# GpSimd without weight splits and residual additions, residual eviction in two VectorE steps, and a third of one modulation summed later

## The chip, the cores and the metric

The kernel runs on one core of one Trainium2 chip. The metric is the device time of one execution in microseconds (us). The engines are named as in the profile: PE (TensorE), DVE (VectorE), ACT (ScalarE), POOL (GpSimd) and SP (SyncE, whose queue issues nearly all DMAs).

## The reference

Two blocks in float32 for 256 tokens of width 2048. The first is a mixer (forgetting attention beside a gated linear recurrence) and a mixture of 16384 small experts; the second is a state-space layer and a sparse attention layer. Each sublayer ends in a residual with a gate that comes from a condition vector:

```python
mod = silu(c) @ w_ada + b_ada                       # [1, 6*2048]: sh1, sc1, ga1, sh2, sc2, ga2
h = rmsnorm(x, g_mix) * (1 + sc1) + sh1
x = x + ga1 * hybrid_mixer(h)                       # w_in, attention and recurrence, w_out
h = rmsnorm(x, g_ffn) * (1 + sc2) + sh2
x = x + ga2 * peer(h)                               # w_q, top-k, u (2048x16384), v (16384x2048)
x = rmsnorm(x, g_final)
for layer in (0, 1):                                # condition vector c_2
    shift, scale, gate = split(silu(c_2) @ mod_w[layer] + mod_b[layer], 3)
    if layer == 1:                                  # shared keys and values: kv_mod_w, w_kv
        shared = nsa_shared_kv(modulate(rmsnorm(x, kv_norm_g), ...))
    h = modulate(rmsnorm(x, norm_g[layer]), shift, scale)
    x = x + gate * (s5_mixer(h) if layer == 0 else nsa_mixer(h, shared))
return rmsnorm(x, final_norm_g)
```

## The kernel before

Activations lie transposed, 16 tiles of 128 channels by 256 tokens, in `x`. Each normed input is kept as a high part in the rounded matmul type and the rest (`xs`). Every weight is used in the same two parts: `half` loads 128x1024 of it by a DMA (tile `raw`, 4 buffers, 512 KB), ACT casts it to `wh` (L342), and a subtraction makes the rest `wl` (L346); `wh` and `wl` have 3 buffers each. A block of 128 output channels (`lin_b`) takes two halves and 16 pairs of matmuls: `wh` with both parts of the input (L357, 512 columns) and `wl` with the high part (L358, 256 columns). Peer's second product (`v_group`) and two others run the other way round (L928 to L930).

Who makes `wl` is set by a share: of each four halves `pool_share` go to POOL, the others to DVE. The share is MP = 1 for w_q, w_k, w_v, MP2 = 2 for w_lx and w_ly, MP3 = 1 for w_out, QP = 3 for peer_w_q, UP = 2 for the first four groups of peer_u, and 0 from then on. That makes 92 splits on POOL and 904 on DVE. DVE's splits are traced with a priority that brings them forward.

A residual eviction (`ev_res`, 16 for each of w_out, ssm_w_out, nsa_w_o) has three engines in a row: ACT scales the first PSUM half (L422), DVE adds the scaled second half (L423), POOL adds the sum to `x` (L424). Behind it ACT squares `x` (L435) and POOL adds the squares (L439); the last square goes to PE, which sums over channels (L445), DVE makes the reciprocal root (L452, L460 to L465: 12 steps, each waiting for the one before), and then norms the input of the next product (L473 to L479). No matmul of the next product can start before that.

The modulations (`gemv`) run in the background, a step at each weight load as the rate allows: SP loads 128x1024 of the matrix (`graw`, 2 buffers, L299), and either PE multiplies, or, where a pool was given by `use_pool`, DVE accumulates into `gacc` (L310 the first, L312 the other 15 of a block of 1024 columns). After 16 steps PE sums `gacc` over its partitions. `self.bg` holds them in order: ga1, ffn, ga2 (w_ada), m0, mkv, m1. `pace(label, loads)` spreads what is left over so many loads, `hold` stops at a label, `need(label)` runs the rest at once. m1 belongs to the last layer; its blocks 0 to 3 are shift and scale, blocks 4 and 5 the gate of the last residual. m0, mkv and m1 are summed in the v stage, where DVE also makes 16 tables for the state-space layer.

The code is traced in this order, and a scheduler then sets the order on every engine's queue by priority and its own forecast of times; the engines take their queues in that order.

Of the kernel before, what the change touches and what calls it, by code (L numbers as in the profile page):

```python
# [9 lines left out]
F = mybir.dt.float32  # L10
# [4 lines left out]
OP = mybir.AluOpType  # L15
# [19 lines left out]
MP = 1  # L35
MP2 = 2
MP3 = 1
# [13 lines left out]
VP = 0  # L51
GP = 1, 0, 1
AHEAD = 200
QP = 3
QS = 3
UP = 2
# [100 lines left out]
class K:  # L157
    def __init__(self, tc, A, dbg=None):
        self.tc, self.nc, self.A = tc, tc.nc, A
        self.dbg = dbg or {}  # L160
        self.full = True
        self.nw, self.pool_share, self.srate = 0, 0, 1
        self.bg, self.side, self.par, self.loads = [], [], [], []
        self.loaded, self.gate, self.gp, self.hold, self.mid = None, None, None, None, False
        self.rate, self.owed, self.sowed, self.towed, self.slow = 1.5, 0.0, 0.0, 0.0, None
# [169 lines left out]
    def half(self, src, i):  # L335
        nc = self.nc
        s = self.sb.tile([128, 1024], F, name="raw", tag="raw", bufs=4)
        with self.after(self.gate):
            self.loaded = nc.sync.dma_start(s, src[:, 1024 * i:1024 * i + 1024])
        h = self.sb.tile([128, 1024], R, name="wh", tag="wh", bufs=3)  # L340
        l = self.sb.tile([128, 1024], R, name="wl", tag="wl", bufs=3)
        nc.scalar.copy(h, s)  # L342
        self.nw += 1
        on_pool = self.nw % 4 < self.pool_share
        with self.tc.high_priority(offset=AHEAD):
            (nc.gpsimd if on_pool else nc.vector).tensor_sub(l, s, h.bitcast(F))  # L346
        return h, l
# [205 lines left out]
    def _mixer(self, x):  # L553
# [6 lines left out]
        for n, w, nb in (("m0", "mod_w0", 6), ("mkv", "kv_mod_w", 4), ("m1", "mod_w1", 6)):  # L560
            if self.full or n == "m0":
                t = cp.tile([128, 8 * nb], F, name=n)
                setattr(self, n, t)
                i, m = {"m0": (0, "mod_b_2"), "m1": (48, "mod_b_2"), "mkv": (0, "kv_mod_b_2")}[n]
# [69 lines left out]
        self.pool_share = MP2  # L634
# [65 lines left out]
        self.pool_share = MP3  # L700
# [47 lines left out]
    def _peer(self, x):  # L748
# [41 lines left out]
        self.pool_share, self.srate = QP, QS  # L790
# [168 lines left out]
        self.pool_share, self.srate = UP, US  # L959
        aps = {}  # L960
        for gi in range(ahead):
            if gi == ahead - 1:
                self.pool_share, self.srate = 0, VS
                self.drain(self.side)
                self.need("ga2")
                self.rate = 0.5
                self.use_pool(None)
                ctx.__exit__(None, None, None)
                aps[0] = self.xs()
                self.side.append(mix(0, gq[0], aps[0]))  # L970
            gq.append(u_group(gi))
# [30 lines left out]
        self.pool_share = 0  # L1002
# [385 lines left out]
    def _nsa(self, x):  # L1388
# [78 lines left out]
        for t in range(2):  # L1467
# [8 lines left out]
                                fill=NEG, base=-31, channel_multiplier=1)  # L1476
        csb = self.ph.tile([128, 2, 128], F, name="csb")
# [81 lines left out]
        for h in range(16):  # L1559
# [11 lines left out]
            self.par.append(head(h, qz, q, sz))  # L1571
        self.drain(self.par)
# [41 lines left out]
```

## Time and profile before

| | |
|---|---|
| median of 3 runs | 3625.65 us (3624.92 to 3626.92) |
| profiled execution | 3617.7 us, span 3616.0 us |
| busy over the span | PE 91%, DVE 73%, ACT 47%, POOL 29% |
| granted PE clock, mean | 0.961 of full speed |
| HBM | 229 GB/s over the span |

The stages, by the first and last loads of their weights in the profiled execution: w_q to w_v 98 to 276 us, w_lx and w_ly 278 to 429, w_out 430 to 567, peer_w_q 567 to 680, peer_u from 681, peer_v 1089 to 2365, ssm_u and ssm_z 2368 to 2696, ssm_w_glu 2699 to 2789, ssm_w_out 2792 to 2879, w_kvt and w_kvn 2882 to 3043, nsa_q and nsa_z 3051 to 3480, nsa_w_o 3481 to 3580. A share of busy time over the whole span hides that PE is full in some of these stages and DVE in others.

### The profile page before, as it was taken

Reading aid. Unit: us, or ns where it says so; the run is one execution under the profiler, and the core shown is the slowest. Engines: PE = TensorE matmul, PEld = TensorE weight load, DVE = VectorE, ACT = ScalarE, POOL = GpSimd, SP = SyncE. Lnnn points to the kernel's source line nnn. Section 1 sums busy time; section 2 is a strip of 40 time slices with the busy share of each in tenths; the row PEclk is TensorE's granted clock in tenths of the full one; section 3 lists DMA queues with packets and bytes.
Section 4 is the critical chain, followed back from the end, with each engine's and each line's share of the span. In section 5 each row is a group of like instructions: output and inputs, shape, how many; then the busy total and the mean of one; then the engine's idle time right before and its main releaser. Section 6 shows DMA issues by size and latency. Waiting matters only on the chain.

```text
span 3616.0 us, 50453 instructions
## 1 busy us (share of the span) xinstructions
PE 3294.4 (91%) x18446; PEld 2726.2 (75%) x18446; DVE 2652.5 (73%) x4072; ACT 1700.7 (47%) x2789; POOL 1066.7 (29%) x892
## 2 busy tenths in 40 slices
PE   4988778999999999999999989988989989999998
PEld 1676666878777777777777777767878878888886
DVE  4778987997657778887777767779886565666665
ACT  1534544455544444554444433354545544555553
POOL 1123345666522121211211233035452320122223
PEclk7999989999999999999999999989999999999999
DMA  9697676567779888888888878744435556444444
GB/s 398 235 301 252 203 234 228 163 223 262 243 250 314 300 281 291 293 285 279 293 286 278 293 268 269 267 158 139 147 127 186 186 167 198 160 155 149 159 143 144
DMA packets 260409, 832.47 MB, mean 230 GB/s; under 512 B 25792, under 2 KB 66880, under 8 KB 257472
## 3 DMA queue, kind: packets, MB, share of 16 engines
q1 hardware_dynamic: 258096, 829.11, 68.0%
q8 instruction: 145, 2.38, 0.3%
q14 instruction: 104, 0.85, 0.1%
q10 hardware_dynamic: 2064, 0.13, 0.0%
HBM read 797.56 MB, written 31.59 MB: 229 GB/s over the span
## 4 chain that ended last, share of the span: by engine, by line
PE 46%; DVE 14%; DMA 13%; issue 6%; POOL 3%; ACT 1%; SPq 0%; DVEq 0%; POOLq 0%; ACTq 0%
PE p L357 22%; PE p L358 11%; DVE wl L346 5%; DMA graw<-mod_w 5%; DMA graw<-kv_mod_w 3%; PE pm L929 2%; PE pm L928 2%; PE pm L930 2%; DVE gacc L312 2%; DMA s5d<-tb 2%; DMA raw<-peer_u 1%; DVE xs L1286 1%; PE pm L882 1%; ACT wh L342 1%; POOL xs L913 1%
## 5 line engine op out<-in xcount | busy, mean ns | idle before, releaser
L357 PE MATMUL p<-xs,wh 128*128 128x512 f32 x5600 | 2038.6, 406 | 43.5 <-DVE xs L476 19.9
L358 PE MATMUL p<-xs,wl 128*128 128x256 f32 x5600 | 1595.6, 285 | 47.6 <-DVE wl L346 40.4
L342 ACT CAST wh<-raw 128x1024 fp32r<-128x1024 f32 x996 | 1038.4, 1048 | 1124.6 <-PE p L357 408.9
L346 DVE TENSOR_TENSOR wl<-raw,wh 128x1024 fp32r<-128x1024 f32 x904 | 1151.4, 1281 | 511.0 <-ACT wh L342 501.4
L357 PEld LDWEIGHTS p<-xs,wh 128*128 128x128 f32 x5600 | 1069.5, 191 | 321.1 <-issue 39.0
L358 PEld LDWEIGHTS p<-xs,wl 128*128 128x128 f32 x5600 | 1078.4, 193 | 74.5 <-DVE wl L346 58.3
L312 DVE SCALAR_TENSOR_TENSOR gacc<-graw,cact,gacc 128x1024 f32<-128x1024 f32 x315 | 448.8, 1425 | 154.5 <-DMA graw<-mod_w 90.2
L929 PE MATMUL pm<-wl,xs 128*128 128x512 f32 x1024 | 411.7, 402 | 25.3 <-DVE wl L346 24.7
L928 PE MATMUL pm<-wh,xs 128*128 128x512 f32 x1024 | 409.4, 400 | 24.2 <-DVE vacc L937 18.8
L930 PE MATMUL pm<-wh,xs 128*128 128x512 f32 x1024 | 405.8, 396 | 0.0
L346 POOL TENSOR_TENSOR wl<-raw,wh 128x1024 fp32r<-128x1024 f32 x92 | 231.8, 2524 | 305.1 <-ACT wh L342 273.1
L909 POOL TENSOR_TENSOR t<-t,t 128x256 f32<-128x256 f32 x128 | 138.3, 1114 | 589.3 <-DMA t<-wd 589.3
L929 PEld LDWEIGHTS pm<-wl,xs 128*128 128x128 f32 x1024 | 196.2, 192 | 85.1 <-DVE wl L346 45.6
L913 POOL TENSOR_TENSOR xs<-t,xs 128x256 fp32r<-128x256 f32 x128 | 150.6, 1207 | 355.0 <-ACT xs L911 354.9
L928 PEld LDWEIGHTS pm<-wh,xs 128*128 128x128 f32 x1024 | 196.0, 191 | 74.9 <-DVE vacc L937 22.1
L930 PEld LDWEIGHTS pm<-wh,xs 128*128 128x128 f32 x1024 | 196.3, 192 | 39.7
L439 POOL TENSOR_TENSOR ssq<-ssq,s 128x256 f32<-128x256 f32 x96 | 105.4, 1107 | 237.7 <-ACT s L435 235.8
L898 ACT ACTIVATE t<-et 128x256 f32<-128x256 f32 x128 | 53.8, 420 | 209.4 <-DVE et L414 209.2
L413 ACT COPY et<-p 128x256 f32<-128x256 f32 x281 | 102.2, 364 | 31.2 <-PE p L358 31.1
L1528 POOL TENSOR_SCALAR t<-t,st 128x128 f32<-128x128 f32 (+1 forms) x64 | 77.6, 1224 | 128.0 <-DVE st L1526 128.0
L872 DVE TENSOR_SCALAR xs<-iof,eT,eT 128x128 f32<-128x128 f32 x192 | 82.2, 487 | 37.9 <-PE pm L882 37.9
L414 DVE TENSOR_TENSOR et<-p,et 128x256 f32<-128x256 f32 x224 | 93.1, 416 | 10.3 <-ACT et L413 10.3
(392 smaller groups left out, 3126.3 us busy)
## 6 DMA issues: line engine op xcount, KB each, us to landing
raw<-peer_u SPq DMA_DIRECT2D x256, 512.0 KB, 5.3
raw<-peer_v SPq DMA_DIRECT2D x256, 512.0 KB, 5.6
graw<-mod_w SPq DMA_DIRECT2D x192, 512.0 KB, 5.6
graw<-w_ada SPq DMA_DIRECT2D x128, 512.0 KB, 4.8
raw<-nsa_z SPq DMA_DIRECT2D x96, 512.0 KB, 3.7
xs<-w_ada SPq DMA_DIRECT2D x16, 2048.0 KB, 13.1
graw<-kv_mod_w SPq DMA_DIRECT2D x64, 512.0 KB, 5.7
raw<-w_out SPq DMA_DIRECT2D x32, 512.0 KB, 5.1
```

What stands on the lines that cost most here:

```text
L312: nc.vector.scalar_tensor_tensor(acc, raw, ck, acc, op0=OP.mult, op1=OP.add)
L342: nc.scalar.copy(h, s)
L346: (nc.gpsimd if on_pool else nc.vector).tensor_sub(l, s, h.bitcast(F))
L357: self.nc.tensor.matmul(p, h[:, sl], x, start=k == 0, stop=False, skip_group_check=True)
L358: self.nc.tensor.matmul(p[:, 1], l[:, sl], x[:, 0], start=False, stop=k == KD - 1, skip_group_check=True)
L413: nc.scalar.copy(t, p[:, 0])
L439: nc.gpsimd.tensor_add(acc[0], acc[0], sq)
L909: nc.gpsimd.tensor_mul(gc, gc, wv[:, c])
L913: nc.gpsimd.tensor_sub(ap[:, c - 2, 1], gs[:, c - 2], ap[:, c - 2, 0].bitcast(F))
L928: nc.tensor.matmul(pp[t], ah, h[:, sl], start=c == 0, stop=False, skip_group_check=True)
L929: nc.tensor.matmul(pp[t], ah, l[:, sl], start=False, stop=False, skip_group_check=True)
L930: nc.tensor.matmul(pp[t], ap[:, c, 1, 128 * t:128 * t + 128], h[:, sl], start=False, stop=c == 7, skip_group_check=True)
```

## The change

POOL makes no `wl` any more: all 996 splits are on DVE, and the shares are gone. A residual eviction is two DVE steps that each add one scaled PSUM half to `x` in place; ACT and POOL have no part in it. Of m1, blocks 4 and 5 get a label of their own, `gate`; it is held back in the v stage, and given free in the last layer, with a pool for its `gacc` there, over 56 loads.

```diff
-MP = 1
-MP2 = 2
-MP3 = 1
-VP = 0
-QP = 3
-UP = 2
...
         nc.scalar.copy(h, s)
-        self.nw += 1
-        on_pool = self.nw % 4 < self.pool_share
         with self.tc.high_priority(offset=AHEAD):
-            (nc.gpsimd if on_pool else nc.vector).tensor_sub(l, s, h.bitcast(F))
+            nc.vector.tensor_sub(l, s, h.bitcast(F))
         return h, l
...
     def ev_res(self, p, x, gate):
         nc = self.nc
-        t, t2 = self.et(), self.et()
-        nc.scalar.activation(t, p[:, 0], AF.Copy, scale=gate)
-        nc.vector.scalar_tensor_tensor(t2, p[:, 1], gate, t, op0=OP.mult, op1=OP.add)
-        nc.gpsimd.tensor_add(x, x, t2)
+        for i in range(2):
+            nc.vector.scalar_tensor_tensor(x, p[:, i], gate, x, op0=OP.mult, op1=OP.add)
...
-                self.bg.append([n, self.gemv(A[w], range(nb), 1, self.col(m, i, 8 * nb), t), 19 * nb + 1])
+            for e, b in ((n, range(nb)),) if n != "m1" else ((n, range(4)), ("gate", range(4, 6))):
+                self.bg.append([e, self.gemv(A[w], b, 1, self.col(m, i, 8 * nb), t), 19 * len(b) + 1])
...
-        if self.full:
-            self.pace("m1", VR)
-        self.pool_share = VP
+        self.pace("m1", VR)
+        self.hold = "gate"
         for gv in range(16):
...
                                 fill=NEG, base=-31, channel_multiplier=1)
+        self.use_pool(self.ph)
+        self.hold = None
+        self.pace("gate", 56)
         csb = self.ph.tile([128, 2, 128], F, name="csb")
...
             self.par.append(head(h, qz, q, sz))
+        self.need("gate")
         self.drain(self.par)
```

The scheduler decides where these steps come to stand. First DVE, at the end of ssm_w_out and the norm that w_kvt waits for (`p` is the PSUM tile of a block, `m` the gate, `s` and `rstd` the tiles of the reciprocal root). Before:

```order
L346 TENSOR_TENSOR wl<-raw,wh 128x1024 x2
L423 SCALAR_TENSOR_TENSOR et<-p_24970,m_993,et 128x256
L452 TENSOR_SCALAR s_25017<-pm 128x256
L460 TENSOR_SCALAR s_25021<-s_25017 128x256
L461 TENSOR_SCALAR rstd<-s_25021 128x256
L463 TENSOR_TENSOR s_25020<-rstd 128x256
```

And of the change, in the same place (lines are those of the changed kernel, some lower than before: L337 is the split, L413 the eviction, L303 and L305 the steps of the modulation):

```order
L413 SCALAR_TENSOR_TENSOR x<-p_24757,m_993,x 128x256 x2
L337 TENSOR_TENSOR wl<-raw,wh 128x1024
L441 TENSOR_SCALAR s_24801<-pm 128x256
L303 TENSOR_SCALAR gacc<-graw,cact 128x1024
L449 TENSOR_SCALAR s_24805<-s_24801 128x256
L305 SCALAR_TENSOR_TENSOR gacc<-graw,cact,gacc 128x1024
L450 TENSOR_SCALAR rstd<-s_24805 128x256
```

Four steps of the gate's second block (L303 and three L305) now stand among the twelve of the reciprocal root; the other twelve stand later, in the norm's end and among the splits of w_kvt. The gate's first block stands earlier than the last layer at all, among the splits of ssm_w_glu, where the queue of before has no such step. DVE of the change there (L405 is an eviction, L1338 belongs to ssm_z):

```order
L1458 MEMSET cm 128x30
L303 TENSOR_SCALAR gacc<-graw,cact 128x1024
L1338 SCALAR_TENSOR_TENSOR t_20235<-et 128x256
L305 SCALAR_TENSOR_TENSOR gacc<-graw,cact,gacc 128x1024
L337 TENSOR_TENSOR wl<-raw,wh 128x1024
L405 TENSOR_TENSOR et<-p_22935,et 128x256
```

All 32 steps of the gate thus left the v stage, and none of them stands in the attention stage proper: PE's sum of the second block is all that comes there. The third place is POOL between w_out and the scores of peer (L424 the residual, L439 the squares, L784 the candidates of the top-k). Before:

```order
L346 TENSOR_TENSOR wl<-raw,wh 128x1024 x2
L424 TENSOR_TENSOR x<-x,et 128x256
L346 TENSOR_TENSOR wl<-raw,wh 128x1024 x4
L784 TENSOR_TENSOR s_5112<-xs 128x256
L346 TENSOR_TENSOR wl<-raw,wh 128x1024 x2
L784 TENSOR_TENSOR s_5177<-xs 128x256
```

And of the change (L428 the squares, L770 the candidates):

```order
L428 TENSOR_TENSOR ssq<-ssq,s_4690 128x256
L428 TENSOR_TENSOR ssq<-ssq,s_4746 128x256
L770 TENSOR_TENSOR s_5064<-xs 128x256
L770 TENSOR_TENSOR s_5129<-xs 128x256
```

The splits stand on DVE now, eight to each four blocks of peer_w_q.

## Rows read from the trace of the kernel before

**Rows 1.** Stretches, all engines: start:end, length, busy us (instructions), clock, DMA, GB/s.
```profile
98.00:302.00 204.00, 183.31 (x1021) 146.62 (x1020) 152.66 (x239) 92.40 (x160) 35.85 (x17) 0.97 0.84 280
302.00:476.00 174.00, 129.94 (x685) 108.84 (x683) 159.43 (x250) 86.61 (x185) 67.54 (x42) 0.90 0.65 212
476.00:586.00 110.00, 88.84 (x488) 74.73 (x489) 85.26 (x95) 45.62 (x72) 59.69 (x38) 0.92 0.77 260
586.00:847.00 261.00, 244.83 (x1529) 205.15 (x1528) 232.79 (x657) 128.57 (x189) 152.86 (x88) 0.96 0.60 199
...
1089.00:2367.00 1278.00, 1202.94 (x5777) 978.40 (x5776) 983.05 (x1076) 571.34 (x760) 262.80 (x231) 0.98 0.84 284
2699.00:2791.00 92.00, 92.00 (x521) 79.62 (x521) 56.31 (x78) 51.02 (x84) 24.15 (x23) 1.00 0.57 183
...
3051.00:3481.00 430.00, 427.04 (x2409) 363.23 (x2408) 269.51 (x483) 229.47 (x500) 93.25 (x87) 1.00 0.48 156
```

The engines of these rows are PE, PEld (weight loads), DVE, ACT, POOL in this order.

**Rows 2.** Splits (L346) by stretch: length, busy us (count) of DVE, POOL.
```profile
98.00:302.00 204.00, 53.33 (x41) 35.46 (x14) 0.97 0.84 280
302.00:476.00 174.00, 20.77 (x18) 44.42 (x16) 0.90 0.65 212
476.00:586.00 110.00, 30.93 (x21) 19.98 (x8) 0.92 0.77 260
586.00:847.00 261.00, 35.43 (x26) 97.30 (x40) 0.96 0.60 199
```

**Rows 3.** DVE lines, 302 to 476 us: busy us, mean ns | idle before.
```profile
L312 DVE SCALAR_TENSOR_TENSOR gacc<-graw,cact,gacc 128x1024 f32<-128x1024 f32 x32 | 58.4, 1826 | 3.1 <-DMA graw<-w_ada 3.1
...
L650 DVE SCALAR_TENSOR_TENSOR s<-lx,cols,s 128x256 f32<-128x256 f32 x24 | 13.5, 565 | 0.2
...
L508 DVE SCALAR_TENSOR_TENSOR et<-et 128x256 f32<-128x256 f32 x8 | 5.3, 668 | 0.6 <-ACT et L507 0.5
...
L512 DVE SCALAR_TENSOR_TENSOR t<-et,t 128x256 f32<-128x256 f32 x8 | 3.3, 412 | 0.0
```

**Rows 4.** Line L312, 98 to 2367 us: shortest/median/longest ns.
```profile
L312 DVE SCALAR_TENSOR_TENSOR gacc<-graw,cact,gacc x315: 1260/1285/3427, 136.1 to 2326.7; 128x1024 f32<-128x1024 f32 x158
```

**Rows 5.** Line L346 on DVE, 2699 to 2897 us, no POOL splits: ns.
```profile
L346 DVE TENSOR_TENSOR wl<-raw,wh x69: 1214/1226/1647, 2702.5 to 2895.1; 128x1024 fp32r<-128x1024 f32 x69
```

**Rows 6.** Line L346 on POOL, whole span: who waited for it (us, times).
```profile
  PEld p L358: 8.1, 5
```

**Rows 7.** Timeline of POOL and of DVE at 430 us: start, length.
```profile
430.59 2.43 POOL L346 TENSOR_TENSOR wl<-raw,wh 128x1024 fp32r<-128x1024 f32 x1 [4.79 <-ACT wh L342]
...
430.68 3.43 DVE L312 SCALAR_TENSOR_TENSOR gacc<-graw,cact,gacc 128x1024 f32<-128x1024 f32 x1
```

**Rows 8.** Groups of the v stage, 1089 to 2367 us: busy, mean | idle before.
```profile
L929 PE MATMUL pm<-wl,xs 128*128 128x512 f32 x1002 | 403.1, 402 | 25.3 <-DVE wl L346 24.7
...
L358 PE MATMUL p<-xs,wl 128*128 128x256 f32 x1304 | 370.9, 284 | 25.5 <-DVE wl L346 25.0
...
L312 DVE SCALAR_TENSOR_TENSOR gacc<-graw,cact,gacc 128x1024 f32<-128x1024 f32 x220 | 295.5, 1343 | 129.5 <-DMA graw<-mod_w 88.0 <-DMA graw<-kv_mod_w 40.2
```

**Rows 9.** Timeline, end of w_out: start, length.
```profile
578.84 4.66 POOL L346 TENSOR_TENSOR wl<-raw,wh 128x1024 fp32r<-128x1024 f32 x2 [0.20 <-ACT wh L342]
...
586.27 1.06 PE L445 MATMUL pm<-s,ones 128*128 128x256 f32 x2
```

**Rows 10.** Timeline, end of ssm_w_out: start, length.
```profile
2896.95 0.70 PE L445 MATMUL pm<-ssq,ones 128*128 128x256 f32 x2
...
2899.04 0.48 DVE L423 SCALAR_TENSOR_TENSOR et<-p,m,et 128x256 f32<-128x256 f32 x1
...
2901.56 0.42 DVE L452 TENSOR_SCALAR s<-pm 128x256 f32<-128x256 f32 x1 [2.04 <-PE pm L445]
```

**Rows 11.** Timeline of DVE, a modulation step inside a reciprocal root.
```profile
478.98 1.28 DVE L312 SCALAR_TENSOR_TENSOR gacc<-graw,cact,gacc 128x1024 f32<-128x1024 f32 x1
480.18 0.42 DVE L463 TENSOR_TENSOR s<-rstd 128x256 f32<-128x256 f32 x1
```

More of the change, by code (lines that the diff above doesn't have):

```diff
@@ L160, in __init__ @@
         self.dbg = dbg or {}
-        self.full = True
-        self.nw, self.pool_share, self.srate = 0, 0, 1
+        self.srate = 1
         self.bg, self.side, self.par, self.loads = [], [], [], []
@@ L560, in _mixer @@
         for n, w, nb in (("m0", "mod_w0", 6), ("mkv", "kv_mod_w", 4), ("m1", "mod_w1", 6)):
[L561 to L564, printed above, removed]
-                self.bg.append([n, self.gemv(A[w], range(nb), 1, self.col(m, i, 8 * nb), t), 19 * nb + 1])
+            t = cp.tile([128, 8 * nb], F, name=n)
+            setattr(self, n, t)
+            i, m = {"m0": (0, "mod_b_2"), "m1": (48, "mod_b_2"), "mkv": (0, "kv_mod_b_2")}[n]
+            for e, b in ((n, range(nb)),) if n != "m1" else ((n, range(4)), ("gate", range(4, 6))):
+                self.bg.append([e, self.gemv(A[w], b, 1, self.col(m, i, 8 * nb), t), 19 * len(b) + 1])
         self.rate, self.hold = R1, "ga2"
-        self.pool_share = MP
         qk = self.xs(F)
@@ L633, in _mixer @@
         self.rate, self.srate = R2, S2
-        self.pool_share = MP2
         lam = self.ph.tile([128, 8], F, name="lam", tag="lam", bufs=1)
@@ L699, in _mixer @@
         self.pace("ffn", 14)
-        self.pool_share = MP3
         for n, p in enumerate(self.lin_bs(A["w_out"], ms, NO)):
@@ L788, in choose @@
                     yield True
-        self.pool_share, self.srate = QP, QS
+        self.srate = QS
         ps = self.lin_bs(A["peer_w_q"], hs)
@@ L958, in _peer @@
         self.side.append(rt)
-        self.pool_share, self.srate = UP, US
+        self.srate = US
         aps = {}
@@ L962, in _peer @@
             if gi == ahead - 1:
-                self.pool_share, self.srate = 0, VS
+                self.srate = VS
                 self.drain(self.side)
@@ L1001, in _peer @@
         self.use_pool(None)
-        self.pool_share = 0
         ctx.__exit__(None, None, None)
```

## The prediction

> **What bounds the kernel now.** I read the stretches of all engines first, since the page's shares (PE 91%, DVE 73%) mix stages with different limits. In [rows 1] PE is busy 244.8 of 261 us in peer_w_q with the top-k, 1202.9 of 1278 in the v stage, all 92 in ssm_w_glu and 427 of 430 in the attention stage: there only PE's own waits can be won. The exception is 302 to 476 us (w_lx, w_ly, the recurrence): PE is busy 130 of 174 us, at a granted clock of 0.90 (some of its time at the lower of the two levels, 1.2 GHz; the v stage, at 0.98, nearly always at 2.4), and DVE 159.4. DVE sets the length there. From 586 to 847 us DVE is nearly as full: 232.8 of 261, 28 us idle. So the question is what 92 splits more cost on DVE in those two stretches, and what comes back.
>
> Second, the splits by stretch [rows 2]: POOL has 14, 16, 8 and 40 of them up to 847 us, and takes 44.42/16 = 2.8 us for one; DVE takes 1.23 where POOL makes none [rows 5]. Third, what POOL's splits do to DVE. From 302 to 476 us the accumulating step L312 has a mean of 1826 ns [rows 3], against a median of 1285 over the stages [rows 4], and at 430 us one takes 3.43 us while POOL splits beside it [rows 7]. So the stretch that DVE sets is long partly because POOL works. Fourth, the groups of the v stage: PE waits for DVE's `wl` 24.7 and 25.0 us [rows 8], and on DVE there the modulation steps stood waiting for `graw` for 128 us: DVE stands in its queue before a step whose load is late, and the splits behind it come late.
>
> **The change, part by part.** The sum is against the profiled execution (3617.7 us, span 3616.0); the median of the runs is 8 us above it, and I apply the difference to the median. About 0.2% (7 us) can be told from no change.
>
> *302 to 476 us.* 16 splits come to DVE: 16 x 1.23 = +19.7 us. Without POOL's splits L312 returns 32 x (1.826 - 1.285) = 17.3 us; L650, taken to fall from 565 to the 412 ns of the equal shape L512, 24 x 0.153 = 3.7; L508 8 x 0.256 = 2.0 [rows 3, 4]: 23.0 back, net -3. The order of the change also moves six of L312's 32 steps to w_out and beyond: -7.7. All of that can't show, since PE, the loads and the recurrence's chain end last in places: I take -5, with -15 (everything, and some for lines not counted) and +5 (nothing returns: 19.7 less the 14.6 us that DVE idles) as ends.
>
> The Trainium skill ("GPSIMD Engine Reference", Key points) says that GpSimd shares its SBUF interfaces with VectorE, with contention for VectorE instructions that have two SBUF inputs. L312 is one and agrees. But a split reads two tiles as well, and DVE's 18 in this stretch have a mean of 20.77/18 = 1.15 us [rows 2], not stretched at all; so the rule doesn't say by itself which instructions pay.
>
> *98 to 302 us.* 14 splits, +17 us, on a DVE that idles 51 us [rows 1]: covered by that idle time. PE's waits for a POOL split, 8.1 us in five places over the whole span [rows 6], go; some become a wait for the next thing. -4 (-8 to 0).
>
> *w_out, 476 to 586 us.* Eight splits (9.8 us), 16 second residual steps at the 0.48 us of L423 [rows 10] (7.7) and the five or so modulation steps moved here (6.4) make 24 us, and DVE idles 110 - 85.3 = 24.7: just covered. At the end two POOL splits (4.66 us, from 578.84) stand ahead of POOL's last residuals, and PE sums only at 586.27 [rows 9]; that goes. -2, from -5 to +6 (the end won in full; the cover used up and a quarter of the 24 us shown).
>
> *peer_w_q, top-k, 586 to 847 us.* The largest doubt. 40 splits are +49 us; 28 are idle. What returns for each split moved is not shown. Below: DVE's own 26 splits there take 35.43/26 = 1.36 us, 0.13 over the 1.23, 3.5 us in all, 0.09 for each POOL split. Above: what L312 pays to 16 splits in the stretch before, 17.3/16 = 1.08 each, 43 us. The top-k's operations are mostly not such steps, so I take a value below the middle, 0.43: 17 back, 49 - 28 - 17 = +4. Ends +18 (0.09) and, at 1.08, 49 - 43 = 6 us within the 28 idle, so that PE's shorter waits gain some: -8, half of the 16 us that PE idles.
>
> *v stage.* L312 ran 220 times there [rows 8], 15 of each block's 16 steps, so there are some 240 steps; 32 leave, 13%. They are worth 13% of PE's 49.7 us of waits, -6.6; and 13% of what the missing 0.02 of clock costs on 1203 us busy (24), -3. Together -10 (0 to -20). The gate's 16.8 MB of loads leave with them.
>
> *Where the 32 steps go.* By the order, 16 stand among the splits of ssm_w_glu: 20 us of DVE, in 92 - 56.3 = 36 idle, DMA at 0.57. By the price that the v stage shows, 49.7/240 = 0.2 us of PE each, +3; to +20 if PE, which idles nowhere there, waits for each in full. Queued behind each such step are a split or an eviction, and PE's next half waits for those. Four more stand inside the reciprocal root before w_kvt, where every step waits for the last and PE for all. Rows show what one does: L312 at 478.98 takes 1.28, and the next step of the root starts only at 480.18 [rows 11]. Four are at most +5; +4. The other twelve lie among the splits of w_kvt, at DMA and DVE shares like ssm_w_glu's, in that +3's bounds.
>
> *Residuals.* At the end of ssm_w_out the next norm starts 4.6 us after the sum of the earlier squares (2896.95 to 2901.56), through ACT, DVE, POOL, ACT and PE, 2.04 of it behind L423 [rows 10]. The chain loses ACT's and POOL's steps for one of DVE, with one less crossing to POOL: half of the 4.6 is ACT, POOL and queueing, so -2; bounds -3 and 0. The same chain ends nsa_w_o, -2. The other residuals are hidden: 16 x 0.48 = 8 us in stages of about 100 us, with DVE near 62% in the stretches on either side [rows 1]; without that cover they would cost those 8 us each.
>
> **Sum.** -5 - 4 - 2 + 4 - 10 + 3 + 4 - 2 - 2 = **-14**: 3602 for the span, 3612 for the median.
>
> **Rivals.**
> 1. *The wait moves and the v stage gives nothing.* PE's next wait is a cast or a load instead of a late split: without the -10, -4, or 3621. For it: in the v stage PE is already 94% busy, DVE's idle is put to loads, and 208 steps stay that wait for loads the same way. Against: the waits are at `wl`, by name.
> 2. *DVE becomes the bound (slower).* Little returns in 586 to 847 us. The place is the 40 splits there: at 0.09 each +18, and with +5 at 302 to 476 us the sum is -14 + 14 + 10 = +10, 3636; with nothing at all 3639. It is measurably slower than before from where a moved split returns under 0.15 us (49 - 28 - 6 = +15, which with the +5 gives -14 + 11 + 10 = +7). For it: DVE's splits there are stretched only 0.13 [rows 2, 5]. Against: the 3.43 us of [rows 7].
> 3. *POOL's splits cost DVE's steps as much in peer_w_q as beside L312.* Then 43 us return there and that term is -8 instead of +4: -26, 3600. For it: the means in [rows 3], where three different lines are stretched. Against: the 1.36 and 1.15 us of DVE's own splits [rows 2]. The Trainium skill's rule above, taken for every instruction with two SBUF inputs, would have it so.
> 4. *The gate's steps block DVE's queue where PE had no gap (slower).* ssm_w_glu and w_kvt pay 1.28 for 16 steps, +20 instead of +3: +3, or 3629; with the twelve in w_kvt as well, +18, 3644. Their loads stand on SP between those of `raw`, and there are two `graw` buffers: a load that waits for one holds up the weights behind it. For it: PE has no slack there to lose from. Against: DMA has 43% to spare, and DVE a third.
> 5. *The v stage is bound by its transfers.* DMA is at 0.84 and 284 GB/s there; 16.8 MB less are 59 us: -14 + 10 - 59 = -63, 3563. For it: the 128 us that DVE waits for `graw`. Against: PE waits some 50 us only, and a stage with PE at 94% can't shorten by more than its 75 us idle.
>
> **How the numbers follow.** Chances: forecast 0.44, rival 1 0.20, rival 2 0.14, rival 3 0.09, rival 4 0.09, rival 5 0.04. The likeliest has 3612, and its own range is 10 us to either side, the bound of the first term and of the v stage's: 3602 to 3622. To hold 8 in 10 the range reaches from rival 3's side, 3590, to 3638, rival 2's, and leaves out rival 5, the far end of rival 4 and the tails. Faster by over 0.2% (under 3618.4): three quarters of the forecast (0.33), a third of rival 1 (0.07), rivals 3 and 5 (0.13), together 0.53, and 0.02 for chance: 0.55. Slower (over 3632.9): most of rival 2 (0.12), half of rival 4 (0.05) and the forecast's tail (0.03): 0.20. Within: the other 0.25.
>
> **What would show it.** No split on POOL. From 302 to 476 us L312's mean falls to about 1.29 us (right) or stays over 1.6 (the contention was another's); the stage is shorter by some 5 us. From 586 to 847 us DVE's share tells the largest term: idle gone and the stage longer by over 10 us, rival 2; idle as before, rival 3. In the v stage PE's waits for `wl`, 49.7 us, fall to about 43; at the same figure, rival 1. PE, which idles nowhere in ssm_w_glu, shows 3 us of idle there, or 20 with rival 4. Between ssm_w_out and w_kvt L303 and three L305 stand between steps of the root, which is 4 us longer, and its start comes 2 us earlier behind the last matmul. I am wrong above all if a split moved to DVE in peer_w_q returns well under 0.4 us, or if the late modulation steps cost PE more than the 0.2 us that they cost it in the v stage.

## The result and the profile after

The changed kernel takes 3567.31 us (median of 4 runs, 3560.96 to 3581.96), 0.9847 times the kernel before (95% interval 0.9816 to 0.9879): 58 us, or 1.5%, faster. A second set of five runs gave 3568.57 (3564.80 to 3578.01), ratio 0.9853 (0.9833 to 0.9873). I forecast 3612, from 3590 to 3638: the sign was right, and the gain is four times what I had worked out. The profiled execution has a span of 3580.2 us, against 3616.0; of the second set, 3564.8.

The page of the profile, first its busy times:

```profile
PE 3275.0 (91%) x18446; PEld 2713.3 (76%) x18446; DVE 2676.1 (75%) x4212; ACT 1685.6 (47%) x2743; POOL 826.9 (23%) x752
```

POOL lost 240 us of work and 140 instructions, and DVE gained only 24 us, though it took over 92 splits (113 us at the 1.23 of [rows 5]) and 48 eviction steps. So something gave DVE more than 100 us back. The windows of the changed kernel, for the stages that [rows 1] shows of before (PE, PEld, DVE, ACT, POOL; clock, DMA share, GB/s): w_q to w_v, w_lx with w_ly, w_out, the v stage, ssm_w_glu, w_kvt with w_kvn, and the attention stage, each from its first load to the next one's:

```profile
99.40:273.30 173.90, 159.28 (x909) 127.45 (x908) 132.89 (x229) 81.55 (x142) 0.39 (x3) 0.96 0.87 291
273.30:402.80 129.50, 119.33 (x651) 100.75 (x650) 116.86 (x214) 77.78 (x166) 17.99 (x21) 0.97 0.72 240
402.80:545.40 142.60, 107.71 (x572) 89.65 (x573) 124.82 (x180) 53.14 (x86) 22.95 (x18) 0.87 0.75 252
1058.70:2318.90 1260.20, 1193.29 (x5764) 977.05 (x5763) 943.76 (x1040) 570.53 (x762) 282.42 (x231) 0.99 0.82 275
2651.60:2748.50 96.90, 92.62 (x522) 79.64 (x521) 77.70 (x95) 50.59 (x83) 28.64 (x22) 1.00 0.80 262
2837.90:3015.40 177.50, 161.14 (x900) 137.24 (x899) 119.94 (x164) 74.46 (x110) 24.44 (x19) 0.96 0.65 214
3015.40:3447.20 431.80, 428.99 (x2420) 363.71 (x2419) 269.26 (x485) 230.10 (x502) 94.22 (x87) 1.00 0.48 155
```

w_lx with w_ly took 151.3 us before by the same loads, and takes 129.5. The v stage went from 1278.2 to 1260.2, in the second profile to 1252.6. Behind it, ssm_w_glu is 4 us longer and w_kvt with w_kvn 9.

DVE's groups from w_lx to w_ly, changed kernel (L305 is L312 of before, L637 is L650, L660 the scan, L708 to L714 the attention's softmax):

```profile
L337 DVE TENSOR_TENSOR wl<-raw,wh 128x1024 fp32r<-128x1024 f32 x32 | 38.7, 1216 | 2.4 <-ACT wh L335 2.3
L305 DVE SCALAR_TENSOR_TENSOR gacc<-graw,cact,gacc 128x1024 f32<-128x1024 f32 x23 | 31.2, 1355 | 2.8 <-DMA graw<-w_ada 2.8
L637 DVE SCALAR_TENSOR_TENSOR s<-lx,cols,s 128x256 f32<-128x256 f32 x24 | 11.4, 473 | 0.0
L660 DVE TENSOR_TENSOR_SCAN t<-t,t 128x256 f32<-128x256 f32 x8 | 8.4, 1107 | 0.3 <-POOL t L659 0.3
L708 DVE SCALAR_TENSOR_TENSOR sl<-pm,cumT,maskb 128x128 f32<-128x128 f32 (+1 forms) x16 | 6.4, 407 | 1.6 <-PE pm L704 1.6
...
L714 DVE TENSOR_SCALAR sl<-sl,st 128x128 f32<-128x128 f32 (+1 forms) x16 | 4.9, 318 | 0.0
```

And five lines of the kernel before in its own w_lx and w_ly (278.5 to 429.8 us); my sum left out the last three:

```profile
L312 DVE SCALAR_TENSOR_TENSOR gacc<-graw,cact,gacc 128x1024 f32<-128x1024 f32 x28 | 48.2, 1721 | 3.5 <-DMA graw<-w_ada 3.5
L346 DVE TENSOR_TENSOR wl<-raw,wh 128x1024 fp32r<-128x1024 f32 x17 | 20.6, 1219 | 9.0 <-ACT wh L342 9.0
L673 DVE TENSOR_TENSOR_SCAN t<-t,t 128x256 f32<-128x256 f32 x8 | 12.0, 1561 | 0.6 <-POOL t L672 0.6
L728 DVE TENSOR_SCALAR sl<-sl,st 128x128 f32<-128x128 f32 (+1 forms) x16 | 11.1, 697 | 0.1
L722 DVE SCALAR_TENSOR_TENSOR sl<-pm,cumT,maskb 128x128 f32<-128x128 f32 (+1 forms) x16 | 6.4, 405 | 0.3 <-PE pm L718 0.3
```

L312's mean fell from 1721 ns there (1826 in [rows 3]) to 1355, the scan's from 1561 to 1107, and L728, a TENSOR_SCALAR with one tensor input (128x128 and 128x256 together), from 697 to 318. The same softmax's L722, which reads PSUM, is the same to 2 ns. So a step with one tensor input was slower beside POOL's splits too, and one that reads PSUM was not. The Trainium skill ("GPSIMD Engine Reference", Key points) names both kinds that pay, VectorE instructions with two SBUF inputs and those in a 2-port performance mode; "VectorE: DVE Perf Modes" (Mode 2×_2P) puts a float32 TENSOR_SCALAR from SBUF to SBUF into that mode and shuts PSUM out of it. The means of L312, L728 and L722 agree with both, but not every such step paid: DVE's own splits, which read two tiles, kept 1219 ns in that stage of the kernel before. My prediction had quoted half of that rule and counted lines of two inputs only.

PE's groups in the v stage, before (1089 to 2367 us; the two lines of [rows 8] belong beside it) and after (1058.7 to 2318.9 us). Before:

```profile
L928 PE MATMUL pm<-wh,xs 128*128 128x512 f32 x1003 | 401.0, 400 | 24.2 <-DVE vacc L937 18.8 <-ACT wh L342 5.4
```

After:

```profile
L914 PE MATMUL pm<-wh,xs 128*128 128x512 f32 x1004 | 397.5, 396 | 11.4 <-ACT wh L335 7.1 <-DVE vacc L923 4.4
L915 PE MATMUL pm<-wl,xs 128*128 128x512 f32 x1003 | 396.9, 396 | 14.0 <-DVE wl L337 14.0
...
L349 PE MATMUL p<-xs,wl 128*128 128x256 f32 x1306 | 375.3, 287 | 41.5 <-DVE wl L337 41.1
```

The waits for `wl`, of which I took 13% away, did not fall: 55.1 us against 49.7. What fell is the wait for `vacc`, DVE's addition that frees PSUM, from 18.8 to 4.4 us, and the mean of a matmul, from 402 to 396 ns at a granted clock of 0.99 for 0.98; PE is busy 1193.3 us for 1202.9. The longest of the kernel before's seven waits for `vacc`, with what stood ahead of the additions in DVE's queue:

```profile
1916.63 1.28 DVE L312 SCALAR_TENSOR_TENSOR gacc<-graw,cact,gacc 128x1024 f32<-128x1024 f32 x1 [0.88 <-DMA graw<-mod_w]
1917.83 1.22 DVE L346 TENSOR_TENSOR wl<-raw,wh 128x1024 fp32r<-128x1024 f32 x1
1920.71 1.28 DVE L312 SCALAR_TENSOR_TENSOR gacc<-graw,cact,gacc 128x1024 f32<-128x1024 f32 x1 [1.67 <-DMA graw<-mod_w]
1921.91 1.22 DVE L346 TENSOR_TENSOR wl<-raw,wh 128x1024 fp32r<-128x1024 f32 x1
1923.05 1.28 DVE L937 TENSOR_TENSOR vacc<-vacc,pm 128x512 f32<-128x512 f32 x2
...
1923.79 0.80 PE L928 MATMUL pm<-wh,xs 128*128 128x512 f32 x1 [3.80 <-DVE vacc L937]
```

A modulation step and a split stand ahead of the additions, and DVE stood still before the step until its load came; all seven waits have such a step close ahead, five of them one that itself waited for `graw`.

DVE at the end of ssm_w_out, which [rows 10] shows of before (L413 the second step and the residual, L441 to L454 the reciprocal root):

```profile
2852.28 1.00 DVE L413 SCALAR_TENSOR_TENSOR x<-p,m,x 128x256 f32<-128x256 f32 x2 [0.54 <-PE p L349]
...
2854.66 0.42 DVE L441 TENSOR_SCALAR s<-pm 128x256 f32<-128x256 f32 x1
2855.00 0.75 DVE L303 TENSOR_SCALAR gacc<-graw,cact 128x1024 f32<-128x1024 f32 x1
...
2855.86 1.28 DVE L305 SCALAR_TENSOR_TENSOR gacc<-graw,cact,gacc 128x1024 f32<-128x1024 f32 x1
...
2859.74 0.43 DVE L454 SCALAR_TENSOR_TENSOR rstd<-s,rstd 128x256 f32<-128x256 f32 x1
2860.80 1.28 DVE L305 SCALAR_TENSOR_TENSOR gacc<-graw,cact,gacc 128x1024 f32<-128x1024 f32 x1 [0.62 <-DMA graw<-mod_w]
2862.00 0.42 DVE L452 TENSOR_TENSOR s<-rstd 128x256 f32<-128x256 f32 x1
```

The root starts 2.6 us after PE's sum of the earlier squares (2852.08) instead of 4.6, and then has the four modulation steps between its own; at one of them DVE waited for `graw` as well. PE's first matmul of w_kvt waited 11.79 us for that norm:

```profile
2866.34 0.77 PE L348 MATMUL p<-xs,wh 128*128 128x512 f32 x1 [11.79 <-DVE xs L468]
```

### The profile page after: what moved, and what is told of

Read it like the earlier page. It is cut to its first block, busy times and chain, and to the rows that moved or that the text cites. A ratio compares the mean times of both kernels' runs of the same rounds, so it can differ in the third digit from the quotient of the medians.

```text
span 3580.2 us, 50406 instructions
## 1 busy us (share of the span) xinstructions
PE 3275.0 (91%) x18446; PEld 2713.3 (76%) x18446; DVE 2676.1 (75%) x4212; ACT 1685.6 (47%) x2743; POOL 826.9 (23%) x752
## 4 chain that ended last, share of the span: by engine, by line
PE 43%; DMA 13%; DVE 11%; issue 6%; POOL 3%; ACT 1%; SPq 0%; DVEq 0%; ACTq 0%; POOLq 0%
PE p L348 17%; PE p L349 9%; DMA graw<-mod_w 8%; DVE wl L337 5%; PE pm L915 4%; PE pm L914 4%; PE pm L916 4%; DMA graw<-kv_mod_w 2%; DVE gacc L305 2%; DVE xs L1270 1%; PE pm L868 1%; ACT wh L335 1%; POOL xs L899 1%; DMA raw<-w_kvt 1%; POOL t L895 1%
## 5 line engine op out<-in xcount | busy, mean ns | idle before, releaser
L337 DVE TENSOR_TENSOR wl<-raw,wh 128x1024 fp32r<-128x1024 f32 x996 | 1261.5, 1273 | 471.5 <-ACT wh L335 461.1
L305 DVE SCALAR_TENSOR_TENSOR gacc<-graw,cact,gacc 128x1024 f32<-128x1024 f32 x315 | 419.5, 1332 | 178.7 <-DMA graw<-mod_w 118.1
L899 POOL TENSOR_TENSOR xs<-t,xs 128x256 fp32r<-128x256 f32 x128 | 161.8, 1294 | 334.7 <-ACT xs L897 334.6
L428 POOL TENSOR_TENSOR ssq<-ssq,s 128x256 f32<-128x256 f32 x96 | 100.3, 1054 | 464.9 <-ACT s L424 463.8
L858 POOL TENSOR_SCALAR xs<-iof,eT,eT 128x128 f32<-128x128 f32 x64 | 98.9, 1552 | 118.0 <-PE pm L868 91.0
L405 DVE TENSOR_TENSOR et<-p,et 128x256 f32<-128x256 f32 x224 | 93.1, 416 | 9.9 <-ACT et L404 9.9
L1270 DVE TENSOR_TENSOR_SCAN xs<-rho,xs 128x128 f32<-128x128 f32 x128 | 74.4, 633 | 14.7 <-POOL xs L1261 14.7
```

What stands on the lines that cost most here:

```text
L305: nc.vector.scalar_tensor_tensor(acc, raw, ck, acc, op0=OP.mult, op1=OP.add)
L337: nc.vector.tensor_sub(l, s, h.bitcast(F))
L899: nc.gpsimd.tensor_sub(ap[:, c - 2, 1], gs[:, c - 2], ap[:, c - 2, 0].bitcast(F))
L1270: nc.vector.tensor_tensor_scan(ma[:, j, i], self.rho[:, g:g + 1].to_broadcast([128, 128]), ma[:, j, i], initial=0.0, op0=OP.mult, op1=OP.add)
```

## The experiments

Each kernel but the last is the changed one with the edit shown. The table gives the time, the ratio to the kernel before, and four stretches of the profiled execution, from the first load of w_q to that of peer_w_q (mixer), to that of ssm_u (peer and v stage), to that of nsa_q, and to the last store. One execution of the profile can be some 10 us off another of the same kernel, as the two rows of the changed kernel show. In seven profiles the work of peer and the v stage is the same by the code (the changed kernel, the splits on POOL up to w_out, the three-engine residual, the idle subtractions, the gate late), and their stretch runs from 1764 to 1781 us; so that one is read within some 10 us, the others within 5.

| kernel | median us | ratio (95% interval) | mixer | peer, v | ssm to w_kvn | attention to end |
|---|---|---|---|---|---|---|
| before | 3625 | 1 | 469.2 | 1800.3 | 683.4 | 561.3 |
| changed | 3567 | 0.9847 (0.9816 to 0.9879) | 446.0 | 1773.5 | 696.5 | 561.1 |
| changed, again | 3569 | 0.9853 (0.9833 to 0.9873) | 441.7 | 1764.4 | 694.9 | 562.0 |
| splits on POOL up to w_out | 3614 | 0.9977 (0.9964 to 0.999) | 477.7 | 1767.7 | 695.8 | 562.4 |
| splits on POOL in peer | 3576 | 0.9867 (0.9847 to 0.9887) | 442.6 | 1770.1 | 695.0 | 562.6 |
| gate in the v stage | 3585 | 0.9895 (0.9877 to 0.9913) | 444.0 | 1792.8 | 679.4 | 561.1 |
| three-engine residual | 3583 | 0.989 (0.9872 to 0.9908) | 437.3 | 1771.6 | 696.5 | 563.3 |
| idle POOL subtractions up to w_out | 3608 | 0.9956 (0.9939 to 0.9972) | 479.3 | 1767.9 | 694.9 | 562.6 |
| splits moved, nothing else | 3592 | 0.9915 (0.9895 to 0.9935) | 444.0 | 1802.2 | 680.2 | 561.6 |
| gate's DVE work in the v stage | 3584 | 0.989 (0.9876 to 0.9904) | 445.0 | 1773.9 | 691.7 | 562.3 |
| gate's loads in the v stage | 3609 | 0.9959 (0.9943 to 0.9975) | 440.6 | 1804.0 | 694.3 | 561.3 |
| gate late | 3570 | 0.9841 (0.9823 to 0.986) | 442.4 | 1781.4 | 679.1 | 566.4 |
| gate late, again | 3561 | 0.9833 (0.9816 to 0.985) | 446.2 | 1774.1 | 678.8 | 566.2 |
| gate late, and a third of m1 later | 3544 | 0.9789 (0.9773 to 0.9805) | 442.7 | 1739.7 | 689.5 | 568.9 |

**The splits of the mixer on POOL again.**

```diff
+        self.nw += 1
+        on_pool = self.nw % 4 < self.pool_share
...
-            nc.vector.tensor_sub(l, s, h.bitcast(F))
+            (nc.gpsimd if on_pool else nc.vector).tensor_sub(l, s, h.bitcast(F))
...
+        self.pool_share = 1      # w_q, w_k, w_v; 2 for w_lx, w_ly; 1 for w_out
```

> The changed kernel with the old shares of splits on POOL up to w_out alone (1, 2, 1 of four); the rest of the change stays. Theory (contention): POOL's splits stretch DVE's steps by about as much as they save DVE, and PE waits for what is late, so all that the trace shows gained up to the end of w_out comes back: -21 us against before there, so the time rises from 3567 by some 20 us to about 3587, ratio to before near 0.990; DVE's accumulating step has a mean of about 1.75 us again in w_lx and w_ly. Rival (the gain there came from the modulation steps that moved to w_out and later, or from the residual): within 7 us of the changed kernel, 3560 to 3574, ratio 0.983 to 0.987.

47 us come back, more than twice what I expected, and the mixer is 32 to 36 us longer: the rival, by which the moved modulation steps or the residual made the gain, is out. The accumulating step has a mean of 1673 ns again in w_lx and w_ly, for the 1750 expected.

**The splits of peer on POOL again** (the same edit, 3 of four for peer_w_q and 2 for the first groups of peer_u).

> The changed kernel with the old shares of splits on POOL in peer_w_q and the first groups of peer_u alone (3 and 2 of four). Theory (contention): each POOL split costs DVE about 1 us there too, as in the mixer; the trace shows 9 us gained from the first load of peer_w_q to the first of peer_v, so the time rises to some 3576, ratio 0.987. Rival (what my prediction took: a POOL split costs DVE less than half of what it saves it there): the splits on POOL are worth 4 us or more, 3563 or below.

The time is that of the first theory (3576), the place is not: the stretch of peer and v has 1770.1 us, within the two profiles of the changed kernel. The other way round, the kernel with nothing but the splits moved has 1802.2 there and the kernel before 1800.3. So these splits cost and gave about the same, though the means of the kernel before are back: the router's TENSOR_SCALAR has 475 ns (542 to 830 us; 355 in the changed kernel, 483 before). Where the 7 or 8 us of time lie stays open; that much is about the noise of two medians.

**The gate in the v stage again.**

```diff
-            for e, b in ((n, range(nb)),) if n != "m1" else ((n, range(4)), ("gate", range(4, 6))):
+            for e, b in ((n, range(nb)),):
...
-        self.hold = "gate"
...
-        self.use_pool(self.ph)
-        self.hold = None
-        self.pace("gate", 56)
...
-        self.need("gate")
```

> The changed kernel with the gate of the last layer summed in the v stage again, all else of the change kept. Theory (the v stage's gain of 18 us in the trace and the 13 us lost again behind it both come from the gate): 3567 + 18 - 13 = 3572, ratio 0.985. Rival (the v stage is bound by its transfers, so the gate's 16.8 MB are worth up to 59 us): 3613, ratio 0.997. Second rival (the v stage gains by something else, and the gate's new places cost 13 us): 3554, ratio 0.980.

18 us slower: more than the first theory had, and far from the transfers' full price. By stretch the gate costs the peer and v stretch 19 to 28 us, and its absence behind it gives 16 to 17 back.

**The residual on three engines again** (`ev_res` as before).

> The changed kernel with the old residual eviction of three engines. Theory: the two-step eviction shortens three chains before a norm by about 2 us each: 3567 + 6 = 3573, ratio 0.986. Rival (it decides no chain, since the sum of squares or the split ahead of it is late): 3567, ratio 0.9847.

15 us slower by the medians, and the stretches don't show where: from the last matmul of w_out to the first of peer_w_q it is 14.7 us for 11.6 and 11.0 in the two profiles of the changed kernel, at the end of the kernel 19.0 for 18.0. That makes 4 to 5; its profiled execution was also its fastest. What the rest is stays open.

**The changed kernel once more.**

> The changed kernel itself, once more, as the mark for the runs that undo one part of it. Expected: 3567 again, between 3558 and 3578, ratio to before 0.982 to 0.988. If it lies at 3575 or more, then undoing the gate (3585) or the residual (3583) cost less than it seemed.

3569 us, so the differences of the runs that undo one part stand.

**The contention alone.** All splits stay on DVE, and POOL makes a subtraction of the same size beside each that it once had, behind a copy of one column that ties it to the split's cast.

```diff
             nc.vector.tensor_sub(l, s, h.bitcast(F))
+        if on_pool:
+            nc.gpsimd.tensor_copy(self.pad[:, :1], h[:, :1].bitcast(F))
+            nc.gpsimd.tensor_sub(self.pad, self.pad, self.pad)
...
```

> The changed kernel, all splits on DVE, with a subtraction of the same size on POOL beside each split that was on POOL up to w_out (some 36, on a tile of its own that nobody waits for): it does no work of the kernel, and only contends. Theory (contention): each stretches DVE's steps by about 1 us, and DVE sets the length from w_lx on: the stages from w_q to w_out are longer by 20 to 36 us, the time near 3592, ratio 0.991. Rival (what POOL's splits cost is that they come late, 2.8 us instead of 1.2, and hold the buffers): within 7 us of the changed kernel.

40 us slower than the changed kernel, for 36 subtractions for which no instruction of the trace waits; the mixer is 33 to 38 us longer, as long as with the real splits on POOL (479.3 and 477.7). The groups of POOL and DVE of this run, from w_lx to w_ly (277.8 to 424.4 us; L306 is the modulation step, L725 the softmax's TENSOR_SCALAR):

```profile
L343 POOL TENSOR_TENSOR dummy<-dummy 128x1024 f32<-128x1024 f32 x15 | 38.9, 2595 | 1.2
```

```profile
L340 DVE TENSOR_TENSOR wl<-raw,wh 128x1024 fp32r<-128x1024 f32 x32 | 42.3, 1328 | 0.5 <-ACT wh L336 0.5
L306 DVE SCALAR_TENSOR_TENSOR gacc<-graw,cact,gacc 128x1024 f32<-128x1024 f32 x23 | 34.7, 1509 | 1.8 <-DMA graw<-w_ada 1.7
L647 DVE SCALAR_TENSOR_TENSOR s<-lx,cols,s 128x256 f32<-128x256 f32 x24 | 13.0, 542 | 0.0
L725 DVE TENSOR_SCALAR sl<-sl,st 128x128 f32<-128x128 f32 (+1 forms) x16 | 10.9, 688 | 0.0
...
L719 DVE SCALAR_TENSOR_TENSOR sl<-pm,cumT,maskb 128x128 f32<-128x128 f32 (+1 forms) x16 | 6.3, 407 | 3.2 <-PE pm L715 3.2
```

The TENSOR_SCALAR is back at 688 ns and the PSUM step unmoved; DVE's splits are stretched too, 1328 for 1216, where before they had hardly been. The scan is not: it has 1098 ns here, so its 1561 in the kernel before comes from something that the idle subtractions don't bring. In all, DVE is busy 421 us of the mixer here and 375 in the changed kernel. So contention alone is shown to cost the mixer as much as the real splits did. That it is all of their cost is not shown, for the two agree in the sum and not by stage: against the changed kernel's first profile w_lx with w_ly is 17 us longer with the idle subtractions and 24 with the real splits, w_out 10 longer with the first and 3 shorter with the second. And with the real splits DVE has 389 us of work in the mixer and idles 31 us more than here. The other expected cost of a POOL split, that it comes late, may make up that part; no run takes it alone.

**Only the splits moved** (the gate in the v stage and the residual as before, with the edits above).

> The kernel before with all splits on DVE and nothing else changed: the residual on three engines, the gate in the v stage. By what undoing the splits cost (47 and 8 us), 3624 - 55 = 3569, ratio 0.985; by what undoing the other two parts cost (18 and 16 us), 3567 + 34 = 3601, ratio 0.994. The parts undone one by one make 89 us together, 32 more than the change, so at least one of these two sums is wrong: which tells whether the splits are worth that much by themselves, or only beside the other parts.

3592 lies between the two sums. With this run the parts can be put in one by one: the splits 3624 to 3592 (-32), the residual to 3585 (-7), the gate to 3568 (-17). Taken out one by one from the changed kernel they are 47 and 8, 15 and 18. So the parts depend on each other: the splits are worth 32 us alone and 55 (47 and 8) beside the other two, some 23 more, while the residual's 7 or 15 us (the gate in the v stage, or away) differ by no more than the noise of these medians. No run has the residual or the gate changed with all splits left on POOL, so the 23 are not taken apart.

**The gate's work and the gate's loads, apart.** First 43 DVE steps of 128x768 in the v stage without loads:

```diff
+        if self.fake and self.nf % 9 == 0:
...
+            nc.vector.scalar_tensor_tensor(self.pad, self.pad, h[:, :1].bitcast(F), self.pad, op0=OP.mult, op1=OP.add)
...
+        self.fake = 43
```

> The changed kernel with 43 accumulating steps of 128x768 on DVE in the v stage, one beside every ninth split, on a tile of their own: the DVE work of the 32 gate steps (some 41 us) without their loads; it is work that the kernel has no use for. Theory (the gate costs the v stage 22 us because its steps fill DVE's queue ahead of the splits and of the additions that free PSUM): the v stage is longer by 15 to 25 us, the time near 3588, ratio 0.990, with PE's wait for vacc up from 4 us towards 18. Rival (it was the 16.8 MB of loads): within 7 us of 3568.

Then 32 loads of 512 KB without steps:

```diff
+        if self.fake and self.nf % 6 == 0:
...
+            raw = self.sb.tile([128, 1024], F, name="graw", tag="graw", bufs=2)
+            self.nc.sync.dma_start(raw, self.A["mod_w1"][128 * k:128 * k + 128, 4096:5120])
...
+        self.fake = 32
```

> The changed kernel with 32 loads of 512 KB more in the v stage, of the size and through the buffers of the gate's loads, that nobody reads: the gate's transfers without its steps. Theory (DVE's queue): within 7 us of 3568, the v stage within 6 us of 1255. Rival (transfers bind there): the v stage longer by 20 us or more, up to 59, the time 3590 to 3627.

My theory fell in part. The loads alone cost 41 us and make the stretch 30 to 40 us longer; the steps alone cost 15, near the 20 that the theory had, but the stretch is only 0 to 10 us longer, though they are 45 us of DVE work, and they don't bring the wait for `vacc`: PE waits 2.1 us for it. PE's groups of the run with the loads in its v stage (1061.9 to 2344.5 us, 1282.6 long):

```profile
L921 PE MATMUL pm<-wl,xs 128*128 128x512 f32 x1003 | 401.7, 400 | 37.1 <-DVE wl L343 36.2
L920 PE MATMUL pm<-wh,xs 128*128 128x512 f32 x1004 | 398.3, 397 | 15.4 <-ACT wh L341 12.3 <-DVE vacc L929 3.1
...
L355 PE MATMUL p<-xs,wl 128*128 128x256 f32 x1289 | 369.3, 286 | 33.0 <-DVE wl L343 32.4
```

With loads added, PE waits 68.6 us for `wl` and 12.3 for `wh`, against 55.1 and 7.1. With loads and nothing else added, a late `wl` is a late weight: DVE makes it as soon as ACT has cast what the DMA brought. That the engine named is DVE hid that.

But neither half is what the gate did there. PE's waits in the v stage, in us:

| v stage of | length | PE busy | wait `wl` | wait `vacc` | wait `wh` |
|---|---|---|---|---|---|
| before | 1278.2 | 1203.1 | 49.7 | 18.8 | 5.4 |
| splits moved, nothing else | 1286.9 | 1206.2 | 51.3 | 20.6 | 8.5 |
| gate in the v stage | 1281.0 | 1201.9 | 52.9 | 17.8 | 7.5 |
| changed | 1260.2 | 1193.3 | 55.1 | 4.4 | 7.1 |
| changed, again | 1252.6 | 1191.6 | 50.1 | 3.7 | 6.7 |
| gate's DVE work | 1260.6 | 1194.3 | 57.8 | 2.1 | 5.4 |
| gate's loads | 1282.5 | 1196.7 | 68.6 | 3.1 | 12.7 |

In the three kernels with the gate there, PE waits no longer for `wl` than without it, and 13 to 17 us longer for `vacc`; loads alone bring the first wait, steps alone neither. The timeline above has what both halves lack: a step that waits for its own load, ahead of the additions. That this is the gate's cost is argued from these waits; no run has such steps and nothing else. What a load costs is not taken apart either. Each waits on SP for one of two `graw` buffers, with the weights behind it: the 32 added loads stood there for 32 us, and SP's waits for those buffers at the modulations' loads fell from 213 us before to 142 with the gate gone. Bytes and this hold are both in the 30 to 40 us.

**The gate truly late.** Each of its loads is tied behind the last weight load traced before it, so the steps come in the attention stage.

```diff
-                    nc.sync.dma_start(raw, w[128 * k:128 * k + 128, c0])
+                    with self.after(self.loaded if self.tail else None):
+                        nc.sync.dma_start(raw, w[128 * k:128 * k + 128, c0])
...
+        self.tail = True
```

> The changed kernel with each load of the gate tied behind the last weight load traced ahead of it, so that its 32 steps truly come in the attention stage and none in ssm_w_glu or w_kvt. Theory (the v stage gains some 22 us by the gate's leaving, and its steps cost 15 us where the scheduler put them, 5 in ssm_w_glu and 10 in the norm and splits of w_kvt): the 15 come back and the attention stage, with DVE at 63% and DMA at 0.48, pays a few: 3567 - 15 + 3 = 3555, ratio 0.981. Rival (PE is full in the attention stage and pays there what it is spared): 3567, the stage longer by some 15 us.

> The kernel with the gate late once more, beside the one above. In its first profile the stages from ssm_u on were 11 us shorter than in the changed kernel, but the stages ahead of them, which are the same work, 17 us longer, at a lower clock in peer_u (0.97 for 0.99). If that was chance, the time is now 3558, ratio 0.982, and the stages up to the v stage are as in the changed kernel; if the order of work ahead is really worse, 3569 again, with peer_u near 401 us.

The stretch from ssm_u to w_kvn is 16 to 18 us shorter than in the changed kernel, the attention stage and the end 4 to 5 longer, as the theory had it; but the ten runs of both together have a median of 3568, and the nine of the changed kernel one of 3568 too. The stretch of peer and v has 1774 and 1781 us, against 1764 and 1774, at work that is the same by the code; two profiles of one kernel differ by about as much there. So the 12 us or so that the later stages save are not shown in the time; peer_u near 401 us was chance, for the second profile has 394.

**A second third of m1 out of the v stage.** The run above, with blocks 2 and 3 held until ssm_w_glu and paced over its loads and those of ssm_w_out.

```diff
-            ... ((n, range(4)), ("gate", range(4, 6))):
+            ... ((n, range(2)), ("m1b", range(2, 4)), ("gate", range(4, 6))):
...
+        self.need("m1")
+        self.use_pool(self.ph)
+        self.hold = "gate"
+        self.pace("m1b", 30)
+        self.tail = True
         for n, p in enumerate(self.lin_bs(A["ssm_w_glu"], ys)):
```

> The kernel of the run with the gate late, with a second third of m1 (blocks 2 and 3) held until ssm_w_glu and summed there and in ssm_w_out, and only blocks 0 and 1 in the v stage. Theory (a step costs PE 0.7 us in the v stage, 0.3 among the splits of ssm_w_glu, 0.15 in the attention stage): 32 x (0.7 - 0.3) = 13 us less than with the gate late alone, 3556, ratio 0.981; the v stage is near 1235 us. Rival (it is only the first third that is dear in the v stage, for the additions that wait behind it are mostly gone by now): the v stage gains under 8 us and ssm_w_glu with ssm_w_out lose 10, so 3570.

3544 us, the fastest kernel here: 17 us under the gate late beside it and 80 under the kernel before (0.9789). Its v stage and its ssm_w_glu with ssm_w_out, by windows:

```profile
1054.40:2280.40 1226.00, 1182.11 (x5752) 971.39 (x5752) 910.40 (x1008) 565.85 (x757) 264.62 (x231) 0.99 0.81 268
```

```profile
2611.50:2803.40 191.90, 185.86 (x1053) 159.00 (x1052) 150.94 (x184) 93.07 (x141) 41.51 (x39) 0.99 0.79 264
```

Another 32 loads with their steps less, and the v stage is 38 us shorter than in the run of the gate late beside it (1263.7), for 12 us more in ssm_w_glu and ssm_w_out (179.9 there). PE's waits fall in all three places: 42.3 us for `wl` where that run has 60.9, 0.8 for 4.0 at `vacc`, and none for `wh`; it is busy 10 us less. So a load of 512 KB with its step is worth 1.2 us in the v stage here, 0.6 to 0.9 for the gate (by the stretch of peer and v), 1.0 to 1.2 for loads alone; and 0.4 in ssm_w_glu and ssm_w_out, where DMA is at 0.61 without them.

## Why the prediction was right and wrong

**302 to 476 us, -5.** The wrong step, and the first to fail: "net -3 ... All of that can't show ... I take -5". I had the mechanism, and measured it on three lines with two inputs (23 us). It acted on steps that the sum left out, such as the TENSOR_SCALAR with one input (697 to 318 ns), and in other stages of the mixer than this one. The mixer as a whole gained 23 to 28 us where I had -5, -4 and -2 in its three pieces, and w_lx with w_ly alone 22 (151.3 to 129.5). The end that I gave as the best, -15, was itself too small. L312's mean did fall, to 1.36 rather than 1.29. The 1.15 us that I read for DVE's own splits is too small, since splits that follow each other overlap in the busy time of [rows 2]; their mean is 1.22.

**98 to 302 and w_out.** w_q to w_v went from 180.4 to 173.9 us and to 171.7 in the second profile, -6.5 and -8.7 for my -4: at the end of its bounds and just beyond. w_out became 5 us longer (137.5 to 142.6; 2 in the second profile) for my -2, within its bounds. The cover of 24.7 us was not what ran out: DVE idles 18 of the 142.6 us, 10 of them for a cast. Why the stage is longer stays open. The chain at its end did lose 3 us.

**peer_w_q and top-k, +4.** "The largest doubt" was none: 0 to 2 us by stretch. The rival of a slower kernel, in which almost nothing returns, is excluded, and the rows that I took as its evidence, DVE's own splits at 1.36, were the wrong rows, since the stretch fell on other steps: the TENSOR_SCALAR of the router had a mean of 483 ns (567 to 847 us) and has 355 (545 to 830 us), and a TENSOR_TENSOR on 128x1024 (`xs` from `posf` and `iof`) fell from 1877 to 1216.

**v stage, -10.** The size was off and so was the path. The gate's leaving is worth 19 to 28 us in that stretch. I priced it by the share of PE's waits at `wl`, which did not fall at all. The term that I put at nothing is PE's wait for `vacc`, which [rows 8] don't show: it fell from 18.8 to 4.4 us. And PE's busy time fell by 10 us where I had 3; 2.6 of it are the gate's own sums on PE (10.9 us before, 8.3 after), which I had left out. I held the rival of the transfers out with 0.04. Loads alone do cost 30 to 40 us there, so its mechanism exists; but they bring another wait than the gate's, so it is not shown to be what the gate cost. Its price, 59, is not reached, since a load costs 0.6 to 1.2 us of the 1.85 that 512 KB take at 284 GB/s. That the time came out within 4 us of that rival's 3563 is chance: its 59 us were to come from the v stage alone, and they came from the mixer and the v stage together. "Against: a stage with PE at 94% can't shorten by more than its 75 us idle" was no argument against 30.

**Where the steps go, +3 and +4, and -2.** ssm_w_glu cost 4 us as I had it. The four steps in the root did as [rows 11] said: from the last matmul of ssm_w_out to the first of w_kvt it is 14.1 and 15.5 us, 11.9 before, and 9.7 with the gate elsewhere: 4 to 6 for the steps, 2 for the shorter residual. The other twelve in w_kvt, which I had put into the bounds of ssm_w_glu's +3, were mis-sized: w_kvt with w_kvn is 9 us longer, 2 to 4 of it at the root, and the stretch from ssm_u to w_kvn 12 to 13, where I had +5.

**Residuals, -2 and -2.** The chain ahead of w_kvt and that ahead of peer_w_q gained 2 and 3 us, the one at the end of the kernel 0.6. By time the part is worth 7 (put in behind the splits) to 15 (taken out of the changed kernel).

Together: splits -32 where the terms say about -7, residual -7 to -15 for -4, gate -17 for -3. All signs of the parts stand and all three sizes were too small; the two large ones are the mixer's splits, with the contention shown, and the gate's leaving the v stage, whose cause is shown only by where PE waits.

## What to carry to other kernels

Work on POOL isn't free for DVE: before giving POOL a large SBUF operation beside a busy DVE, compare the means of all DVE groups in and out of its company, those with one input too, and not only the splits' own. A wait named after the engine that makes a tile can be a late transfer two steps earlier: add loads without work, and work without loads, and see which of them brings back the wait that the change took away; here neither did. And background loads with their steps did better here where DMA stood at 0.61 than at 0.82, even though PE idles nowhere there.

## What was not expected of the hardware

A POOL subtraction on 128x1024 floats (2.0 to 2.6 us by stage) costs DVE more than 1 us in the mixer: with 36 of them, and a copy of one column beside each, DVE was busy 47 us more and the mixer 33 to 38 us longer, though nobody waited for them. A TENSOR_SCALAR with a single tensor input is stretched to twice its time (318 to 688 ns) and an accumulating step to as much as 3.43 us [rows 7], while the step that reads PSUM keeps its time to 1% (405 to 407 ns). And in the v stage, where DMA is at 0.82 to 0.84, 32 loads of 512 KB that nobody reads made it 22 to 30 us longer (1282.6 for 1260.2 and 1252.6), and the whole 41, though PE is 93 to 95% busy there.
